# Parameter arithmetic at the head of the program, and S5's absolute phases in a half tile of their own, in a two-layer trunk of mixers and gated MLPs

## The chip, the cores and the metric

The kernel runs on one core of a Trainium2 chip. The metric is the device time of one execution in microseconds, taken as the median of several runs. One more execution was recorded by the hardware profiler; its trace gives the start and the length of each instruction. TensorE (PE) does matmuls and transposes, its weight loads are listed as PEld, VectorE is DVE, ScalarE is ACT, GpSimd is POOL, and SyncE (SP) issues nearly all DMAs.

## What is computed

The reference is a trunk of two layers on 1024 tokens of 1024 features, all in float32. Layer 0 mixes with RG-LRU (512 wide) and S5 (256 wide), layer 1 with HGRN2 and dilated attention, and each layer ends in a gated MLP with a short convolution. What the change touches are quantities of the parameters alone:

```python
# S5, per group and state
dt = jnp.exp(log_dt)[:, None]
mag = jnp.exp(ar * dt)
abar_re = mag * jnp.cos(ai * dt); abar_im = mag * jnp.sin(ai * dt)
# RG-LRU, per channel
log_a = (RG_C * r) * jax.nn.log_sigmoid(lam)
# HGRN2, per channel
lb_p = jax.nn.softmax(hg_lower, axis=0); lb_all = jnp.cumsum(lb_p, axis=0) - lb_p[0]
```

The S5 scan is done in blocks: the kernel forms cosines and sines of the phases `iota * angle` for 128 block positions, as sin(2 pi x) and sin(pi/2 - 2 pi |x|) of a phase x wrapped to half a turn either way.

## The kernel before

Tokens lie in 8 tiles of 128. In `load_x` SP issues the loads: a tile `par0` of all small parameters first, then the gain row, x tile by tile with weights in between, and S5's and RG-LRU's small weights. The small weights and the parameter results share wide tiles called arena, from which `tiny` hands out columns. One DVE instruction there needs no load (the memset of `ones`).

`start` then normalises the tiles. PE spreads the gain row over the partitions, DVE copies it out (L205, `gpre`), and each tile goes through a row sum of squares on ACT (L142), four dependent small DVE instructions for the reciprocal root (L134 to L137, behind L133), the product on DVE (L148, `xn`), 8 transposes on PE (L235, `pt`), and for each half a high part on ACT (L89, `yh`) and a low part on DVE (L90, `yl`). Projection matmuls (`pj`, L279 to L281) of the first two weight units run between the tiles. Inside `start` the order of PE, ACT and DVE is fixed by hand (`in_order`); everything else is ordered when the program is built, by a list scheduler that takes what it reckons to be ready, work that was traced earlier first. Once built, an engine runs its own list in order.

Three blocks of parameter arithmetic run on DVE, on 4 to 16 columns an instruction. `s5_params` begins with an exponential (`pexp`, 18 instructions, L766 to L778) for dt and the product t0 (L793), goes on with the exponential of t0 (mag) and the angles (th), then powers and tables. `rg_params` (L1036 to L1052) holds a `pexp` and a series for the logarithm. Both are traced behind the first part of the projections, and `hg_params` (L1366 to L1378, with a `pexp`) in layer 1. All three may not be issued on DVE ahead of the instruction that `self.dve_start` names, the last DVE instruction of the third tile's split (`tc.issue_after`).

Then `s5_lift` builds the tables of a quarter of S5's groups: products on POOL (L894 to L896), phase steps on DVE (L908 to L911 with `wrap`, L782 and L783), and on ACT Sin (L915), Abs in place (L916) and Sin (L917). There are four lifts. RG-LRU's convolution steps on DVE are L1061, and its gates use Sigmoid, Exp, Tanh and Sqrt on ACT; a change between some of these functions needs a table load on ACT.

Of the kernel before, what the change touches and what calls it, by code (L numbers as in the profile page):

```python
# [13 lines left out]
AF = mybir.ActivationFunctionType  # L14
ALU = mybir.AluOpType
# [30 lines left out]
class Trunk:  # L46
# [118 lines left out]
    def load_x(self, x, g):  # L165

        nc, a = self.nc, self.a
        self.hs = []
        self.par0 = self.small([P, 93], "par0", bufs=1)
        nc.sync.dma_start(self.par0, a["par0"])  # L170

        self.grow = self.T("grow")[:1]
        nc.sync.dma_start(self.grow, g.unsqueeze(0))
        self.ones = self.T("ones")[:1, :P]
        nc.vector.memset(self.ones, 1.0)
        self.gpre = self.cp.tile([P, 1024], F32, tag="g0", name="gpre")
        self.bx, self.cx = self.tiny("s5bx", 512), self.tiny("s5cx", 512)
        self.rgw, self.wglu = self.tiny("rgw", 1024), self.tiny("wglu", 512)
        for t in range(NT):
            if t % 2 == 0:  # L180
                h2 = self.T2("h")
            h = h2[:, t % 2]
            nc.sync.dma_start(h, x[t * P:(t + 1) * P, :])
            self.hs.append(h)
            if t == 0:
                nc.sync.dma_start(self.cst, a["cst"][:, :C_BIAS])
            if t == 1:
                self.fetch(2)
            if t == 5:
                nc.sync.dma_start(self.bx, a["s5_b"])  # L190
                nc.sync.dma_start(self.cx, a["s5_c"])
        nc.sync.dma_start(self.rgw, a["rg_w"])
        nc.sync.dma_start(self.wglu, a["s5_wglu"])
        self.rgw = self.rgw.rearrange("p (j c m) -> p j c m", j=2, c=4)
        self.wglu = self.wglu.rearrange("p (k c) -> p k c", k=2)

    def start(self):

# [586 lines left out]
    def s5_params(self):  # L785
        nc, a, v = self.nc, self.a, self.nc.vector
        tt = v.tensor_tensor
        G = 16
        par = self.par0
        ar, ai, ldt = par[:, 0:16], par[:, 16:32], par[:, 32:48]  # L790
        dt, mag, th, k, t0 = (self.tiny(f"s5{x}") for x in ("dt", "mag", "th", "k", "t0"))
        self.pexp(dt, ldt, 16)
        tt(t0, ar, dt, op=ALU.mult)  # L793
        self.pexp(mag, t0, 16)
        tt(th, ai, dt, op=ALU.mult)
        v.tensor_scalar(k, th, INV2PI, MAGIC, op0=ALU.mult, op1=ALU.add)
# [9 lines left out]
        sn, cs = self.tiny("s5sn"), self.tiny("s5cs")  # L806
# [12 lines left out]
        for m, n in ((1, 1), (2, 2), (4, 4)):  # L819
            br = pr[:, m:m + 1].to_broadcast([P, n, G])  # L820
            bi = pi[:, m:m + 1].to_broadcast([P, n, G])
            x, y = pr[:, 1:1 + n], pi[:, 1:1 + n]
# [57 lines left out]
    def s5_lift(self, q):  # L880

        nc, v = self.nc, self.nc.vector
# [22 lines left out]
        x, y = xy[:, 0], xy[:, 1]  # L905
# [6 lines left out]
        self.wrap(x, y)  # L912
        two = self.T2("s5csz")
        cs = w["cs"] = D4(two[:, 0])
        nc.scalar.activation(cs[:, 1], x, AF.Sin, scale=6.2831850)  # L915
        nc.scalar.activation(x, x, AF.Abs)  # L916
        nc.scalar.activation(cs[:, 0], x, AF.Sin, scale=-6.2831850, bias=self.halfpi)  # L917

        C1, C2 = (self.cx[:, j * 256:(j + 1) * 256].rearrange("p (g q) -> p g q", g=16) for j in range(2))
        z = w["z"] = D4(two[:, 1])  # L920
# [186 lines left out]
    def params0(self):  # L1107
        self.ahead(3)
        with self.tc.issue_after(self.dve_start):
            self.s5_params()  # L1110
            self.rg_params()
        self.gens.append([self.s5_all_tables(), 1])

    def s5_all_tables(self):
# [398 lines left out]
    def layer1_mixer(self, pend, hsrc, hdst):  # L1513
        nc = self.nc
        self.gens = []
        self.tick = self.drive(self.gens)
        self.qkv, self.og, self.ml, self.mix = {}, {}, {}, {}
        self.hq, self.ho, self.hsg = {}, {}, {}
        with self.tc.issue_after(self.dve_start):
            self.hg_params()  # L1520
        self.hg_values(pend)
        self.proj_chunks([self.da_job(g, kd, c) for g in range(3) for kd in "qkv" for c in range(2)], iter(pend), self.tick, parts=(512, 512))
        scm = self.T2("scm")
        self.scm = [scm[:, j].rearrange("p (t s) -> p t s", t=8) for j in range(2)]
        nc.gpsimd.memset(scm, 0.0)
        self.seg = self.cp.tile([P, 1024], F32, tag="g0", name="seg")
        nc.gpsimd.tensor_copy(self.seg.rearrange("p (n s) -> p n s", s=64), self.cst[:, C_SEG:C_SEG + 64].unsqueeze(1).to_broadcast([P, 16, 64]))

        jobs = [f(h) for h in range(4) for f in (self.hg_qjob, self.hg_fjob)] + [self.hg_gjob(h) for h in range(4)]
        self.proj_chunks(jobs, pend, self.tick, 4, (512, 512))  # L1530
        while self.gens:
            self.tick()
        return self.mix_out(1, 6, hsrc, hdst)
# [110 lines left out]
```

## Time and profile before

| | us |
|---|---|
| median of 3 runs | 2216.42 |
| lowest and highest | 2215.26, 2219.97 |
| profiled execution, its own time | 2214.25 |
| its span, first to last instruction | 2212.5 |
| PE busy | 2124.8 |
| DVE busy | 1589.3 |
| ACT busy | 1043.2 |
| POOL busy | 106.1 |

The busy times are sums over the span and lie beside one another. A stretch is read from the time of its own engines: one that is busy for the whole of it can set its length. In a timeline the distance from start to start is what an instruction takes of its engine's time; its own length can be longer, since the next may start before it has ended. The granted clock is the share of full speed that TensorE was given.

### The profile page before, as it was taken

To read this page: it belongs to the slowest core of one execution; us is meant where nothing else is said; L and a number is where in the kernel's file an instruction comes from. 1 tells how busy PE (TensorE), PEld (TensorE's weight loads), DVE (VectorE), ACT (ScalarE), POOL (GpSimd) and SP (SyncE) were. 2 spreads that over 40 slices of the span, in tenths; PEclk is the share of its full clock that TensorE was granted. 3 is DMA by queue.
4 is the path that set the end of the run, shared out by engine and by line. 5 is a ranking of instruction groups with operands and counts; after the bars stand their busy time and mean duration, and the time that the engine had idled before them with its cause. 6 is when DMAs were issued, how large, how long until landed. Compare 5 with 4: busy or idle time off the path is not lost.

```text
span 2212.5 us, 25422 instructions
## 1 busy us (share of the span) xinstructions
PE 2124.8 (96%) x10088; PEld 1720.5 (78%) x10088; DVE 1589.3 (72%) x2091; ACT 1043.2 (47%) x1437; POOL 106.1 (5%) x93
## 2 busy tenths in 40 slices
PE   7899989999999999999999999999899999999997
PEld 6677868888887888878877877778688888878886
DVE  8887687777777797971233366677877777778888
ACT  5548445444444444540233376444444544444443
POOL 0550000000000000000000000420000000000000
PEclk9999999999999999999999999999999999999999
DMA  4012322222213530330111111434122221234404
GB/s 164 12 35 98 116 103 86 78 85 86 86 71 119 211 140 23 116 141 29 39 34 54 47 35 29 118 112 157 53 86 86 86 86 70 83 141 163 153 10 152
DMA packets 53896, 198.82 MB, mean 90 GB/s; under 512 B 7045, under 2 KB 8133, under 8 KB 51218
## 3 DMA queue, kind: packets, MB, share of 16 engines
q1 hardware_dynamic: 52130, 193.49, 24.3%
q0 software_dynamic: 1504, 3.46, 0.6%
q8 instruction: 79, 1.29, 0.2%
q14 instruction: 39, 0.32, 0.0%
q10 hardware_dynamic: 144, 0.26, 0.0%
HBM read 154.60 MB, written 41.99 MB: 89 GB/s over the span
## 4 chain that ended last, share of the span: by engine, by line
PE 81%; DVE 12%; ACT 4%; issue 2%; DMA 1%; SPq 0%; DVEq 0%; ACTq 0%
PE ac L279 11%; PE ac L281 11%; PE ac L280 11%; PE pd L280 7%; PE pd L281 7%; PE pd L279 7%; PE pj L279 5%; PE pj L280 5%; PE pj L281 5%; PE bb L281 2%; PE bb L280 2%; PE bb L279 2%; DVE wl L90 1%; PE ppt L1263 1%; PE pi L281 1%
## 5 line engine op out<-in xcount | busy, mean ns | idle before, releaser
L279 PE MATMUL pj<-yh,wh 128*128 128x512 f32 (+1 forms) x672 | 267.5, 398 | 6.3 <-ACT s5uf L84 4.4
L280 PE MATMUL pj<-yl,wh 128*128 128x512 f32 (+1 forms) x672 | 262.0, 390 | 1.0 <-DVE yl L90 1.0
L281 PE MATMUL pj<-yh,wl 128*128 128x512 f32 (+1 forms) x672 | 260.2, 387 | 0.0
L280 PE MATMUL pd<-dwl,dgh 128*128 128x512 f32 x528 | 205.9, 390 | 0.8 <-DVE dwl L90 0.8
L281 PE MATMUL pd<-dwh,dgl 128*128 128x512 f32 x528 | 205.6, 389 | 0.0
L279 PE MATMUL pd<-dwh,dgh 128*128 128x512 f32 x528 | 205.3, 389 | 0.0
L279 PEld LDWEIGHTS pj<-yh,wh 128*128 128x128 f32 x672 | 129.7, 193 | 34.9 <-ACT s5uf L84 4.5
L279 PE MATMUL ac<-ah,w2h 128*128 128x512 f32 x352 | 143.8, 409 | 7.3 <-ACT ah L89 7.3
L280 PEld LDWEIGHTS pj<-yl,wh 128*128 128x128 f32 x672 | 129.6, 193 | 27.2 <-issue 4.1
L281 PEld LDWEIGHTS pj<-yh,wl 128*128 128x128 f32 x672 | 129.1, 192 | 24.7 <-issue 0.7
L279 PE MATMUL ac<-ah,w4h 128*128 128x512 f32 x352 | 142.2, 404 | 6.1 <-ACT val L489 3.8
L280 PE MATMUL ac<-al,w2h 128*128 128x512 f32 x352 | 139.4, 396 | 1.8 <-DVE al L90 1.8
L281 PE MATMUL ac<-ah,w2l 128*128 128x512 f32 x352 | 139.4, 396 | 0.0
L280 PE MATMUL ac<-al,w4h 128*128 128x512 f32 x352 | 137.6, 391 | 0.0
L281 PE MATMUL ac<-ah,w4l 128*128 128x512 f32 x352 | 137.3, 390 | 0.0
L280 PEld LDWEIGHTS pd<-dwl,dgh 128*128 128x128 f32 x528 | 99.1, 188 | 22.1 <-DVE dwl L90 1.6
L279 PEld LDWEIGHTS pd<-dwh,dgh 128*128 128x128 f32 x528 | 99.1, 188 | 20.8
L281 PEld LDWEIGHTS pd<-dwh,dgl 128*128 128x128 f32 x528 | 99.1, 188 | 20.4
L515 ACT ACTIVATE tg<-tg 128x1024 f32<-128x1024 f32 x44 | 46.7, 1061 | 137.9 <-DVE tg L448 137.9
L89 ACT ACTIVATE dwh<-dw 128x1024 fp32r<-128x1024 f32 x66 | 69.7, 1056 | 86.6 <-PE pd L280 72.8
L446 ACT ACTIVATE tv<-val,cw 128x1024 f32<-128x1024 f32 x44 | 54.7, 1243 | 108.8 <-DVE val L453 108.8
L90 DVE TENSOR_TENSOR w1l<-wr,w1h 128x1024 fp32r<-128x1024 f32 x44 | 53.9, 1225 | 64.1 <-ACT w1h L89 64.1
(444 smaller groups left out, 5023.4 us busy)
## 6 DMA issues: line engine op xcount, KB each, us to landing
wr<-in_WU_dram SPq DMA_DIRECT2D x88, 512.0 KB, 4.3
raw<-in_W_dram SPq DMA_DIRECT2D x56, 512.0 KB, 3.8
gd<-tv SPq DMA_DIRECT2D x44, 512.0 KB, 2.6
dg<-gd SPq DMA_DIRECT2D x20, 1024.0 KB, 5.2
dw<-in_WD_dram SPq DMA_DIRECT2D x20, 1024.0 KB, 7.9
h<-h SPq DMA_DIRECT2D x28, 512.0 KB, 4.2
h<-hn SPq DMA_DIRECT2D x20, 512.0 KB, 2.9
h<-in_x_dram SPq DMA_DIRECT2D x16, 512.0 KB, 4.9
```

Source lines behind the costliest of these rows:

```text
L89: self.nc.scalar.activation(hi, src, AF.Copy)
L90: self.nc.vector.tensor_tensor(lo, src, hi.bitcast(F32), op=ALU.subtract)
L279: mm(out, lhsT=lh, rhs=rh, start=first, stop=False, skip_group_check=chain)
L280: mm(out, lhsT=lh, rhs=rl, start=False, stop=False, skip_group_check=chain)
L281: mm(out, lhsT=ll, rhs=rh, start=False, stop=last, skip_group_check=chain)
L446: nc.scalar.activation(t0, src, AF.Identity, scale=cw[:, c, 2:3], bias=cw[:, c, 3:4])
L515: nc.scalar.activation(tg, tg, AF.Gelu_apprx_tanh)
L1263: nc.tensor.transpose(pt[:, hp, j], sc[:, hp, j], self.ident)
```

## The change

`load_x` now ends with dt's `pexp`, t0, `hg_params` and `rg_params`, on columns of the same arena, without the `issue_after`. They are traced ahead of `start` and are not part of its fixed order. `s5_params` takes dt and t0 from there, and `rgp` is set earlier since `rg_params` reads it. In `s5_lift` the Abs is traced first and writes into `y`, the half tile that the wrapping used before and that nothing needs any more; the two Sin follow, one of x and one of y.

```diff
--- before.py
+++ after.py
@@ -193,6 +193,13 @@
         nc.sync.dma_start(self.wglu, a["s5_wglu"])
         self.rgw = self.rgw.rearrange("p (j c m) -> p j c m", j=2, c=4)
         self.wglu = self.wglu.rearrange("p (k c) -> p k c", k=2)
+
+        dt, t0 = self.s5dt = self.tiny("s5dt"), self.tiny("s5t0")
+        self.pexp(dt, self.par0[:, 32:48], 16)
+        nc.vector.tensor_tensor(t0, self.par0[:, 0:16], dt, op=ALU.mult)
+        self.rgp = self.par0[:, 48:80].rearrange("p (c j) -> p c j", c=4)
+        self.hg_params()
+        self.rg_params()
 
     def start(self):
 
@@ -788,9 +795,8 @@
         G = 16
         par = self.par0
         ar, ai, ldt = par[:, 0:16], par[:, 16:32], par[:, 32:48]
-        dt, mag, th, k, t0 = (self.tiny(f"s5{x}") for x in ("dt", "mag", "th", "k", "t0"))
-        self.pexp(dt, ldt, 16)
-        tt(t0, ar, dt, op=ALU.mult)
+        mag, th, k = (self.tiny(f"s5{x}") for x in ("mag", "th", "k"))
+        dt, t0 = self.s5dt
         self.pexp(mag, t0, 16)
         tt(th, ai, dt, op=ALU.mult)
         v.tensor_scalar(k, th, INV2PI, MAGIC, op0=ALU.mult, op1=ALU.add)
@@ -912,9 +918,10 @@
         self.wrap(x, y)
         two = self.T2("s5csz")
         cs = w["cs"] = D4(two[:, 0])
+
+        nc.scalar.activation(y, x, AF.Abs)
         nc.scalar.activation(cs[:, 1], x, AF.Sin, scale=6.2831850)
-        nc.scalar.activation(x, x, AF.Abs)
-        nc.scalar.activation(cs[:, 0], x, AF.Sin, scale=-6.2831850, bias=self.halfpi)
+        nc.scalar.activation(cs[:, 0], y, AF.Sin, scale=-6.2831850, bias=self.halfpi)
 
         C1, C2 = (self.cx[:, j * 256:(j + 1) * 256].rearrange("p (g q) -> p g q", g=16) for j in range(2))
         z = w["z"] = D4(two[:, 1])
@@ -1108,7 +1115,6 @@
         self.ahead(3)
         with self.tc.issue_after(self.dve_start):
             self.s5_params()
-            self.rg_params()
         self.gens.append([self.s5_all_tables(), 1])
 
     def s5_all_tables(self):
@@ -1516,8 +1522,6 @@
         self.tick = self.drive(self.gens)
         self.qkv, self.og, self.ml, self.mix = {}, {}, {}, {}
         self.hq, self.ho, self.hsg = {}, {}, {}
-        with self.tc.issue_after(self.dve_start):
-            self.hg_params()
         self.hg_values(pend)
         self.proj_chunks([self.da_job(g, kd, c) for g in range(3) for kd in "qkv" for c in range(2)], iter(pend), self.tick, parts=(512, 512))
         scm = self.T2("scm")
```

## Rows read from the trace of the kernel before

**Rows 1.** The page's part 2, PE and DVE: busy tenths in 40 slices of 55.3 us.

```profile
PE   7899989999999999999999999999899999999997
...
DVE  8887687777777797971233366677877777778888
```

**Rows 2.** Three stretches: length, busy us of each engine (instructions), granted clock, DMA share, GB/s.

```profile
24.90:43.00 18.10, 14.07 (x115) 13.35 (x114) 18.10 (x130) 10.79 (x22) 0.00 (x0) 1.00 0.00 1
...
57.00:71.00 14.00, 11.50 (x61) 9.65 (x60) 14.00 (x26) 0.00 (x0) 12.48 (x11) 1.00 0.00 0
71.00:80.00 9.00, 6.04 (x24) 5.07 (x24) 6.85 (x9) 6.90 (x9) 2.69 (x5) 0.62 0.06 13
```

**Rows 3.** Waits from 20 to 60 us, PE: engine line <- who: us in total, times, longest.

```profile
PE pt L235 <- DVE xn L148: 6.2, 5, 2.6
```

**Rows 4.** Timeline, DVE, 21-43 us: start us, us, engine line op out<-in xcount [idle before <-releaser].

```profile
21.80 1.28 DVE L148 SCALAR_TENSOR_TENSOR xn<-h,rn,gpre 128x1024 f32<-128x1024 f32 x1
...
24.35 0.69 DVE L90 TENSOR_TENSOR yl<-pt,yh 128x512 fp32r<-128x512 f32 x1 [0.66 <-ACT yh L89]
24.96 0.17 DVE L766 TENSOR_SCALAR pe<-par 128x16 f32<-128x16 f32 x1
25.03 0.16 DVE L1366 TENSOR_TENSOR hgm<-par 128x4 f32<-128x4 f32 x1
...
26.70 1.28 DVE L148 SCALAR_TENSOR_TENSOR xn<-h,rn,gpre 128x1024 f32<-128x1024 f32 x1
...
36.32 1.28 DVE L148 SCALAR_TENSOR_TENSOR xn<-h,rn,gpre 128x1024 f32<-128x1024 f32 x1
...
42.73 0.16 DVE L1043 TENSOR_TENSOR arena<-arena 128x4 f32<-128x4 f32 x1
42.84 1.28 DVE L148 SCALAR_TENSOR_TENSOR xn<-h,rn,gpre 128x1024 f32<-128x1024 f32 x1
```

**Rows 5.** Timeline, DVE, 57 to 80 us.

```profile
57.30 0.15 DVE L1046 SCALAR_TENSOR_TENSOR arena<-arena 128x4 f32<-128x4 f32 x1
...
59.92 1.25 DVE L1046 SCALAR_TENSOR_TENSOR arena<-arena 128x4 f32<-128x4 f32 x1
...
61.90 1.27 DVE L1061 SCALAR_TENSOR_TENSOR rgu<-pj,par,rgu 128x1023 f32<-128x1023 f32 x1
...
70.39 0.30 DVE L1052 TENSOR_SCALAR arena<-arena 128x4 f32<-128x4 f32 x3
...
79.74 1.60 DVE L908 TENSOR_TENSOR s5x<-cst,arena 128x512 f32<-128x512 f32 x1
```

**Rows 6.** The parameters' tile (par): its DMA's issue, and its time to landing.

```profile
L170 SPq DMA_DIRECT2D par<-in_par_dram x1: 389/389/389, 0.7 to 0.7; - x1
...
DMA to landing us min/median/max: 1.8/1.8/1.8
```

**Rows 7.** Timeline, DVE, the opening.

```profile
6.47 1.23 DVE L205 COPY gpre<-pg 128x1024 f32<-128x1024 f32 x1 [5.42 <-PE pg L204]
...
7.86 0.16 DVE L135 TENSOR_TENSOR tn<-tn,vn 128x1 f32<-128x1 f32 x1
8.06 0.16 DVE L136 TENSOR_TENSOR tn<-tn,qn 128x1 f32<-128x1 f32 x1
```

**Rows 8.** Timeline, POOL, at 59.6 us.

```profile
59.60 1.54 POOL L896 TENSOR_TENSOR s5tm<-s5tm 128x512 f32<-128x512 f32 x1
```

**Rows 9.** Timeline, ACT, 87 to 96 us.

```profile
87.44 1.28 ACT L915 ACT_TABLE_LOAD   x1
89.11 0.64 ACT L915 ACTIVATE s5csz<-s5x 128x512 f32<-128x512 f32 x1 [0.38 <-DVE s5x L783]
...
92.21 0.61 ACT L916 ACTIVATE s5x<-s5x 128x512 f32<-128x512 f32 x1
...
93.88 1.28 ACT L917 ACT_TABLE_LOAD   x1
...
95.92 1.28 ACT L1079 ACT_TABLE_LOAD   x1
```

## The prediction

> **What bounds the kernel now.** I read the page's 40 slices first. A slice is 55 us. TensorE (PE) stands at 9 tenths or more nearly everywhere; of the slices with work of this change it is lower in the first two, with 7 and 8, while VectorE (DVE) stands at 8 in the first three [rows 1]. So in the opening some 110 us, and hardly behind them, a DVE instruction can be worth its time. Then I read the stretches. From 24.9 to 43 us DVE has no idle time at all (18.10 of 18.10) and PE works 14.07; from 57 to 71 us DVE is again full, 14.00 of 14.00, with PE at 11.50 [rows 2]. The waits between 20 and 60 us say who waits: PE's transposes wait five times, 6.2 us in all, for the DVE instruction that writes the normalised tile xn (L148) [rows 3]. So the path of these 50 us runs through DVE, and the small parameter instructions stand on it.
>
> **What the edit moves.** 86 DVE instructions: the exponential for dt (18) and t0 (1), hg_params (28), rg_params (39). No DMA moves, and nothing on SP's or POOL's queue. In the kernel before 72 of them start between 24.96 and 42.73 us [rows 4]; summing start to next start they take 6.03 us, 0.084 each. One more lies alone, and the last 13, the end of rg_params, lie from 57.30 to 70.39 us and take 5.39 us [rows 5]. The new place is the start of DVE's queue. The parameters' DMA is issued at 0.7 us and lands 1.8 us later [rows 6], at 2.5 us; DVE stands idle for 5.42 us until the gain row's copy into gpre (L205) starts at 6.47 [rows 7]. So 4.0 us of the hole can be used.
>
> **Term 1, the tiles of 25 to 43 us.** Not all of the 6.03 us comes back, since part of it filled holes. I take a tile's period from a stretch without these instructions: from one xn (21.80) to the end of the second yl (24.96, the idle 0.66 of the row at 24.35 included) is 3.16 us [rows 4], and the four dependent steps of a row's reciprocal root come at 0.20 each, 0.8 us [rows 7]. That makes 4.0 us. With the instructions it is 4.81 (26.70 to 36.32 is two periods) [rows 4]. Saved: 1.74 less 0.8 in the piece from 24.96 to 26.70, twice 0.8, and in the last period (36.32 to 42.84, 6.52 us, of which a weight's low part takes 1.22) 1.3. Sum **3.8 us**. S5's own chains of mag and th, some 25 instructions that stay, find the 0.66 us hole and the gaps of 0.12 us between dependent steps; if they find none, 25 x 0.08 = 2.0 us are lost again (lower end 1.8). The upper end is the whole 6.0. What is late next is PE itself: its 14.07 us are 4.0 short of the stretch [rows 2], which agrees with 3.8.
>
> **Term 2, the 13 instructions of 57 to 71 us.** Four of them, on 4 columns each, last over 1 us: the one at 59.92 takes 1.25 [rows 5], and ends at 61.17, when POOL's instruction of 59.60 ends (61.14) [rows 8]. So they wait for POOL to be done with something both use. If that wait passes on to the next DVE instruction, only 14 x 0.08 = 1.1 us are saved; if it goes with them, 5.4. For the first: in the second lift, where no small instruction stands in between, the phase product (L908) itself takes 1.60 us [rows 5]. For the second: here the first convolution's three steps (L1061) stand between the phase steps; the one at 61.90 reads 1023 columns from PSUM in 1.27 us [rows 5] while POOL works nearly throughout, 12.48 of 14 us [rows 2], so such steps can fill POOL's turns. I take **3.5**, somewhat nearer to this second end, for these three.
>
> **Term 3, S5's Abs ahead of both sines.** In lift 1 Sin, Abs and Sin are apart, with Exp and Tanh in between, and ScalarE (ACT) loads four tables, at 87.44, 93.88 and 95.92 us and once in between, 1.28 us each [rows 9]. With the absolute phases in their own half the second sine no longer waits on an Abs just issued, so the two sines can stand side by side: two loads fewer, 2.56 us. Against that, the first load (87.44) lay within a wait for DVE that lasted until 89.11 [rows 9]; Abs runs under any table here (92.21, behind an Exp and with no load of its own), so the load will come behind Abs, after the wait: 1.28 us given back. Net **1.3 us** on ACT, which works without a gap here from 89.11 to the load at 95.92 [rows 9]; ends 2.6 (the load stays hidden) and -1.3 (lifts 0 and 2, where the sines already stand together, gain nothing and only lose the hidden load). I credit nothing for lift 3.
>
> The Trainium skill (ScalarE: Activation LUTs, What ACT_TABLE_LOAD costs) puts a switch of sets at about 2.66 us, the load and a drain behind it; by that two switches are worth 5.3 us and the sum below would be 2.8 larger. The trace differs: the load at 93.88 and the Sin behind it leave room for the next load after 2.04 us (95.92) [rows 9], so there is no such drain.
>
> **Term 4, the opening.** DVE takes its instructions in queue order, so the change adds a wait: the gpre copy, the first reciprocal roots and the first xn are queued behind instructions that wait for the parameters' DMA, and PE's first transposes wait for xn. That wait is over at 2.5 us; what costs is the number of instructions ahead of the copy. Independent chains interleave at about 0.08 us an instruction (the 72 above at 0.084; 24.96 and 25.03) [rows 4]; one chain alone goes at 0.20 (7.86, 8.06) [rows 7]. Three chains are now ready at once. In the kernel before two such chains and a reciprocal root filled DVE without a hole, and the work ready earliest and traced earliest went first; here that is the three chains. So I expect the copy where the shortest chain ends: 3 x 19 = 57 instructions, 4.6 us, to 7.1 us: 0.6 late. The other 29 go into gaps of the first norms; I put another 0.6 for those that don't fit. **1.2 us lost.** Ends: 0 (49 or fewer are ahead: 49 x 0.08 = 3.9), and 4.6 if all 86 are ahead (19 rounds of 0.24, then 20 of 0.20, is 8.6 us, to 11.1).
>
> **Sum:** 3.8 + 3.5 + 1.3 - 1.2 = 7.4 us. All of it stands before 100 us. Behind it the work hangs together by engines and buffers and not by absolute times, so I carry it to the end whole. The profiled execution took 2214.25 us (span 2212.5, 1.75 around it), 2.2 below the median of 2216.42; I take 7.4 from the median: 2209.0.
>
> **Rivals.** (a) *The queue's head is slow: slower than before.* The 86 run chain by chain ahead of the copy: at the dependent 0.20 us they take 17.2 us, from 2.5 to 19.7, and the copy is 13.2 late; less the 8.6 of terms 1 to 3, 4.6 slower: 2221.0. It decides once the copy is later than 15 us. Against it: before, the dt and hg chains alternate one by one from the start [rows 4]. The Trainium skill (VectorE: DVE Perf Modes, The DRAIN you can't avoid) has a rule that speaks for it: a DVE instruction starts only when the one ahead has left the pipe. Here instructions of 0.16 to 0.17 us start 0.07 apart (24.96, 25.03) [rows 4], so independent ones overlap and the trace doesn't bear the rule out. Chance 0.09.
>
> (b) *Half of it is hidden anyway.* The lower ends of terms 1 and 2 with no gain on ACT and 1.2 lost: 1.8 + 1.1 - 1.2 = 1.7: 2214.7. For it: DVE's holes between yl halves are real, and in lift 1 the waits on POOL fall on whoever is there. Chance 0.19.
>
> (c) *It gives more: the clock too.* From 71 to 80 us the granted clock is 0.62, while PE works 6.04 of 9 us after idle time in the 14 us before [rows 2]; at full clock some 3.4 us of these 9 come back. With the upper ends of terms 1 and 2 halfway (4.9, 4.5) and term 3, less 1.2, plus 3.4: 12.9: 2203.5. Chance 0.20.
>
> (d) *The edit doesn't do what it says:* the moved instructions stay where they were because the queue puts the copy and the norms ahead of them. Then only term 3 is left: 2215.1. Against it: hg_params, traced only for layer 1, ran at 25.03 us [rows 4], as soon as it was allowed to. Chance 0.05.
>
> **How the numbers follow.** Forecast 2209.0, chance 0.47, with (a) to (d) as above. This kernel's measurement can tell about 0.2%, 4.4 us: faster means under 2212.0. Faster: the forecast and (c), 0.67. Same: (b) and (d), 0.24. Slower: 0.09. Range: all upper ends with the clock (6.0 + 5.4 + 2.6 + 3.4 = 17.4) reach 2199.0, all lower ends (1.8 + 1.1 - 1.3 - 4.6 = 3.0 lost) 2219.4; I take 2200 to 2218, which leaves out (a) and the corners.
>
> **What would show it.** Term 4: the start of L205's copy, 6.5 to 7.5 us, with some 57 small instructions ahead. Term 1: xn's periods at 4.0 to 4.2 us, the last xn near 40 us, and PE's 6.2 us of waits for L148 mostly gone. Term 2: the last phase step of lift 0 (L783, right behind the row at 70.39) 6 to 8 us earlier, and which instruction now lasts over 1 us while POOL works. Term 3: two Sin behind one load in lift 1. Wrong I would be if L205 starts beyond 11 us, if the lost time on POOL's turns reappears in full on the phases, or if the gain at 100 us is not there at 220.

## The result and the profile after

| | before | after |
|---|---|---|
| median, us | 2216.35 | 2229.84 |
| lowest and highest, us | 2215.26, 2219.97 | 2226.25, 2232.07 |
| profiled execution, its own time, us | 2214.25 | 2228.48 |
| its span, us | 2212.5 | 2226.7 |

The change makes the kernel slower: 1.0054 times the time of before, 95% interval 1.0043 to 1.0066, where 2209.0 us was forecast. The profiled executions differ by 14.2 us, and that is the sum to explain. Here is where it arises, as the start of the same instruction in both traces:

| start of | before, us | after, us | later by |
|---|---|---|---|
| the gain row's copy (gpre) | 6.47 | 7.51 | 1.0 |
| the first low part (yl) | 12.83 | 20.19 | 7.4 |
| the last of the eight xn | 42.84 | 51.32 | 8.5 |
| POOL's first product of lift 1 | 79.56 | 83.97 | 4.4 |
| the first gate's second Sigmoid | 86.31 | 102.59 | 16.3 |
| RG-LRU's first scan | 102.0 | 116.67 | 14.7 |
| the first matmul into pd, behind layer 0's mixers | 217.2 | 233.0 | 15.8 |
| the first gelu of the first MLP | 345.0 | 362.1 | 17.0 |
| the last row sum of the program (into hn) | 2200.6 | 2214.8 | 14.2 |

So 7.4 us are lost in the opening and 1.1 more up to the last xn, 4.1 are won between the last xn and lift 1, 11.9 are lost at one Sigmoid, and behind 100 us the lateness moves by 3 us at most. First the page's part 2, PE and DVE in 40 slices, to be read beside [rows 1]:

```profile
PE   6889989999999999999999999899899999999997
DVE  7787688777777797981234257677877777778888
```

PE's first slice falls from 7 to 6, and the rest hardly moves. Then stretches, with the columns of [rows 2]; the first is the tiles (24.9 to 43 us there, moved on by 8.5), the second the one behind POOL:

```profile
33.40:51.50 18.10, 14.37 (x107) 13.82 (x105) 14.24 (x58) 11.04 (x22) 0.00 (x0) 0.91 0.00 1
...
65.00:79.00 14.00, 12.06 (x64) 10.15 (x62) 13.93 (x17) 2.33 (x5) 13.01 (x12) 1.00 0.00 0
```

DVE's work in the tiles fell from 18.10 to 14.24 us with 72 instructions fewer (58 instead of 130), by about what Term 1 forecast as saved time, and the tiles take no less than before: DVE is now idle for the difference. PE's waits between 20 and 60 us for xn, 6.2 us in [rows 3], are mostly still there:

```profile
PE pt L242 <- DVE xn L148: 5.0, 3, 2.8
```

(Three are left of five, also when the window is moved on by 8.5 us; at two of the tiles PE itself comes late, which the section on the prediction takes up.)

**The opening**, DVE's timeline, against [rows 7]:

```profile
2.56 0.17 DVE L773 TENSOR_SCALAR pe<-par 128x16 f32<-128x16 f32 x1 [1.51 <-DMA par<-in_par_dram]
...
7.43 0.17 DVE L1384 TENSOR_SCALAR oml<-lb 128x4 f32<-128x4 f32 x1
7.51 1.22 DVE L212 COPY gpre<-pg 128x1024 f32<-128x1024 f32 x1
...
13.85 0.17 DVE L785 TENSOR_TENSOR arena<-pe,peki 128x16 f32<-128x16 f32 x1
13.94 0.16 DVE L1043 TENSOR_SCALAR arena<-par 128x4 f32<-128x4 f32 x1
...
18.34 1.54 DVE L1053 SCALAR_TENSOR_TENSOR arena<-arena 128x4 f32<-128x4 f32 x8
...
20.19 0.68 DVE L90 TENSOR_TENSOR yl<-pt,yh 128x512 fp32r<-128x512 f32 x1
```

DVE begins when the parameters land, at 2.56 us as [rows 6] gave it, and the chains of dt and hg run before the copy (45 instructions; the heads of three chains, 57, were forecast). But dt's last step, the first that writes to the arena (13.85), stands behind two xn and a weight's low part, and behind it, in front of the first yl, t0 and 36 of the 39 instructions of rg_params: from 13.94 to 20.19 us DVE works through what is nearly one dependent chain, at 0.20 us a step. ACT waits for it 7.49 us:

```profile
20.91 0.60 ACT L89 ACTIVATE yh<-pt 128x512 fp32r<-128x512 f32 x1 [7.49 <-DVE yl L90]
```

One row of SP's queue says what is special about the arena: a weight that lies in the same tile is loaded late, the last of that tile's loads.

```profile
12.75 0.33 SPq L193 DMA_DIRECT2D arena<-in_s_wglu_dram  x1
```

**Lift 1**, ACT's timeline, against [rows 9]:

```profile
87.95 1.11 ACT L1078 ACTIVATE rgg<-rgpg,par 128x1024 f32<-128x1024 f32 x1 [3.92 <-PE rgpg L1076]
98.10 0.63 ACT L922 ACTIVATE s5x<-s5x 128x512 f32<-128x512 f32 x1 [9.03 <-DVE s5x L790]
98.75 1.28 ACT L923 ACT_TABLE_LOAD   x1
100.04 0.63 ACT L923 ACTIVATE s5csz<-s5x 128x512 f32<-128x512 f32 x1
100.58 0.70 ACT L924 ACTIVATE s5csz<-s5x,halfpi 128x512 f32<-128x512 f32 x1
101.30 1.28 ACT L1078 ACT_TABLE_LOAD   x1
102.59 1.11 ACT L1078 ACTIVATE rgg<-rgpg,par 128x1024 f32<-128x1024 f32 x1
```

Abs and the two Sin stand together behind one load, as forecast. They also stand between the gate's two Sigmoids, and ACT is idle 9.03 us until DVE has the phases. In the kernel before, both Sigmoids came first:

```profile
84.53 1.11 ACT L1071 ACTIVATE rgg<-rgpg,par 128x1024 f32<-128x1024 f32 x1 [4.66 <-PE rgpg L1069]
86.31 1.11 ACT L1071 ACTIVATE rgg<-rgpg,par 128x1024 f32<-128x1024 f32 x1 [0.67 <-PE rgpg L1069]
```

And the phases themselves got later: their first product takes 4.78 us where [rows 5] have 1.60, and they end at 98.06 us. Behind the Sigmoid the gate's product on DVE waits 5.08 us for it, and the first scan follows. DVE's timeline of after:

```profile
83.91 4.78 DVE L914 TENSOR_TENSOR s5x<-cst,arena 128x512 f32<-128x512 f32 x1
...
97.37 0.69 DVE L790 TENSOR_TENSOR s5x<-s5x 128x512 f32<-128x512 f32 x1
...
103.74 1.23 DVE L1081 TENSOR_TENSOR rgg<-rgg,rgu 128x1024 f32<-128x1024 f32 x1 [5.08 <-ACT rgg L1078]
...
116.67 2.29 DVE L1090 TENSOR_TENSOR_SCAN rgg<-rgg,rgt 128x1024 f32<-128x1024 f32 x1
```

In the kernel before the phases end at 89.08 us:

```profile
87.41 1.67 DVE L783 TENSOR_TENSOR s5x<-s5x 128x512 f32<-128x512 f32 x1
...
102.02 2.29 DVE L1083 TENSOR_TENSOR_SCAN rgg<-rgg,rgt 128x1024 f32<-128x1024 f32 x1
```

### The profile page after: what moved, and what is told of

Read it like the earlier page. It is cut to its first block, busy times and chain, and to the rows that moved or that the text cites. A ratio compares the mean times of both kernels' runs of the same rounds, so it can differ in the third digit from the quotient of the medians.

```text
span 2226.7 us, 25418 instructions
## 1 busy us (share of the span) xinstructions
PE 2127.5 (96%) x10088; PEld 1722.2 (77%) x10088; DVE 1597.3 (72%) x2091; ACT 1043.1 (47%) x1437; POOL 103.5 (5%) x93
## 4 chain that ended last, share of the span: by engine, by line
PE 80%; DVE 13%; ACT 5%; issue 2%; DMA 1%; DVEq 0%; ACTq 0%; SPq 0%
PE ac L286 11%; PE ac L288 11%; PE ac L287 11%; PE pd L287 7%; PE pd L286 7%; PE pd L288 7%; PE pj L287 5%; PE pj L286 5%; PE pj L288 5%; PE bb L288 2%; PE bb L286 2%; PE bb L287 2%; DVE wl L90 1%; PE ppt L1269 1%; PE pi L288 1%
```

## The experiments

The theory from the two traces: (A) the second Sigmoid is late because lift 1's three activations stand ahead of it on ACT and wait for DVE; (B) the opening is late because results share a tile with a late load, so they are placed behind it and in front of yl. Rivals: the moved instructions cost by their number; or the Abs edit costs by itself.

All runs in one table: starts against the kernel before in the profiled executions, us later (negative is earlier); the median against the one of before on the same chip; the ratio with its 95% interval. No kernel leaves work out.

| kernel | first yl | last xn | lift 1, POOL | 2nd Sigmoid | first scan | first pd | first gelu | last hn | median | ratio |
|---|---|---|---|---|---|---|---|---|---|---|
| after | 7.4 | 8.5 | 4.4 | 16.3 | 14.7 | 15.8 | 17.0 | 14.2 | +13.5 | 1.0054 [1.0043, 1.0066] |
| abs_only | 0.1 | 0.9 | 0.1 | 12.7 | 11.0 | 12.6 | 12.4 | 12.3 | +11.1 | 1.0044 [1.0029, 1.0059] |
| par_only | 7.5 | 8.3 | 4.3 | 12.4 | 9.4 | 12.6 | 12.7 | 16.5 | +11.0 | 1.0043 [1.0029, 1.0057] |
| rg_back | 1.3 | 1.4 | 1.1 | 13.7 | 12.1 | 11.7 | 11.7 | 12.0 | +9.8 | 1.0041 [1.0023, 1.0059] |
| late_sin | 7.5 | 8.2 | 6.6 | 6.0 | 6.9 | 8.1 | 9.5 | 12.8 | +10.3 | 1.0042 [1.0025, 1.0059] |
| abs_late | 0.1 | 0.1 | 2.0 | 1.7 | 3.5 | 3.6 | 7.2 | 7.7 | +6.0 | 1.0024 [1.0013, 1.0035] |
| rg_own | 0.0 | 1.0 | -2.4 | 5.1 | 2.2 | 3.3 | 5.1 | 2.0 | +4.2 | 1.0021 [1.0012, 1.0031] |
| rg_own_late | 0.1 | 1.1 | 0.5 | 2.2 | -1.3 | 2.1 | 2.1 | 2.3 | +3.6 | 1.0017 [1.0006, 1.0027] |
| own_tile | 3.2 | 3.8 | -0.2 | 11.7 | 10.1 | 11.6 | 11.7 | 8.2 | +5.9 | 1.0028 [1.0019, 1.0038] |
| late1 | 0.1 | 0.6 | 2.3 | 1.8 | -1.7 | 4.1 | 7.6 | 4.9 | +4.1 | 1.0020 [1.0010, 1.0029] |
| abs_late1 | 0.1 | 0.9 | 1.9 | 2.1 | 3.4 | 5.0 | 5.1 | 5.3 | +3.9 | 1.0019 [1.0009, 1.0028] |
| rg_own_late1 | 0.0 | 0.8 | -1.7 | -2.9 | -4.1 | 1.1 | 4.5 | -1.6 | +0.5 | 0.9998 [0.9989, 1.0008] |
| own_tile_late1 | 3.1 | 4.1 | 0.0 | -1.0 | 0.7 | 3.8 | 5.4 | 5.3 | +2.9 | 1.0007 [0.9995, 1.0018] |
| abs_lateq1 | 0.1 | 0.9 | 1.9 | 2.2 | 3.4 | 4.9 | 8.3 | 8.9 | +5.3 | 1.0027 [1.0015, 1.0038] |
| rg_own_lateq1 | 0.1 | 1.5 | -1.1 | -3.8 | -3.5 | -2.7 | -1.0 | -0.4 | -2.0 | 0.9991 [0.9982, 1.0001] |
| rg_own_abs_lateq1 | 0.2 | 0.3 | -2.3 | -2.5 | -4.5 | -3.3 | 0.2 | 4.4 | -1.8 | 0.9993 [0.9984, 1.0003] |
| own_tile_lateq1 | 3.1 | 3.1 | -0.9 | -0.3 | 0.6 | 1.7 | 3.1 | 6.2 | +1.3 | 1.0003 [0.9994, 1.0013] |

Each row of starts is one execution. The last column of starts differs from the first gelu's by 6.1 us less to 4.2 more within one kernel's trace; this comes in layer 1, between 1270 and 1480 us, and goes with no edit. The column of the first gelu holds up to 3.6 us that come from the clock and not from the edit (last section). The columns up to the first pd carry the argument.

### Each half of the change, and each half undone

abs_only is the kernel before with the change's three activation lines; par_only has all of the change but these; rg_back and late_sin are the changed kernel with one move taken back or one added:

```diff
 # rg_back: after, with rg_params at its old place
-        self.rg_params()            # in load_x
             self.s5_params()
+            self.rg_params()
 # late_sin: after, the three activations issued in s5_tables
-        nc.scalar.activation(y, x, AF.Abs)          # ... and both Sin, in s5_lift
+        w["xy"] = x, y
+        nc.scalar.activation(y, x, AF.Abs)          # ... and both Sin, in s5_tables
```

> The kernel before with the Abs alone changed (into the other half tile, ahead of both Sin); the parameters stay where they were. Theory A: what costs is ACT's queue. In the order built, the Abs and both Sin of lift 1 stand ahead of the second gate's Sigmoid and wait for DVE's phases; before, that Sigmoid ran at 86.3 us and the phases were ready at 89.1, so it comes at about 89.1 + 0.6 + 1.3 + 1.3 + 1.3 = 93.6, 7 us late: 2222 to 2225. Theory B (ACT only saves loads, the loss is all in the opening): 2215, and the Sigmoid at 86 to 88.

> The changed kernel with Sin, Abs in place, Sin as they were before; the parameters moved. Theory A: opening 7.4 us late as in the changed kernel, some 4 us won back between 52 and 82 us, and since the first Sin of lift 1 still stands ahead of the second Sigmoid in the order built, some 4 to 7 more are lost there: 2223 to 2228. Theory B (only the opening counts): 2216.4 + 7.4 - 4 = 2220.

> The changed kernel with rg_params back at its old place behind s5_params; dt, t0 and hg_params stay moved, the Abs stays ahead. Opening theory: the first yl comes at 14 us and not at 20.2, as rg_params' chain no longer stands ahead of it; the last xn at 44 us and not 51.3. Theory A then still loses some 7 us at lift 1: 2223 to 2226. Theory B (the opening is all): 2217 to 2218.

> The changed kernel with each lift's three activations traced with its tables, behind the gates, and nothing else changed: in the order built both Sigmoid of the first gates now stand ahead of lift 1's Abs. Theory A: opening 7.4 us late, 4 won back by 82 us, the second Sigmoid right behind the first: 2219 to 2222. Rival (the late Sigmoid is a consequence and not a cause, DVE's phases behind POOL set the time): still 2228 to 2231.

The two halves lose 11.1 and 11.0 us alone and 13.5 together, since either of them makes the second Sigmoid late. abs_only loses 12.6 us between lift 1's start (0.1 late) and the second Sigmoid (12.7), which is enough for its 11.1 us of median; 7 were expected, and the rest is phases that end 5.4 us later. par_only and rg_back fall within theory A's times. abs_only's ACT timeline shows the same queue as after, with no parameter moved:

```profile
85.63 1.11 ACT L1072 ACTIVATE rgg<-rgpg,par 128x1024 f32<-128x1024 f32 x1 [5.32 <-PE rgpg L1070]
94.47 0.63 ACT L916 ACTIVATE s5x<-s5x 128x512 f32<-128x512 f32 x1 [7.73 <-DVE s5x L783]
...
98.97 1.11 ACT L1072 ACTIVATE rgg<-rgpg,par 128x1024 f32<-128x1024 f32 x1
```

par_only has the old order of the three, and its second Sigmoid is 12.4 late all the same, 8.1 of them behind lift 1's start: here the first Sin alone stands between the Sigmoids. So the Abs is not needed for the fault: moving parameters alone can turn the two round when the program is built. By what reckoning the scheduler does it is not traced. rg_back takes the opening's loss from 7.4 to 1.3 and puts rg_params' instructions back among the tiles: its DVE is busy for 16.08 of the 18.1 us from 24.9 (80 instructions, against 58 in after). From the fourth xn to the last it takes 21.1 us (23.13 to 44.26), before takes 21.0, and own_tile_lateq1 (below), without those instructions and with PE as early there as in before, 21.0 as well (24.92 to 45.90): their number costs nothing there. late_sin frees the Sigmoid, which comes 6.0 late instead of 16.3, and still gains only 3.2 us of median: it also loses the 2.2 us by which lift 1 now starts later, so the test was not clean, and its 2226.3 lies between the times of the theory and of the rival.

### The tile, and the queue

abs_late and rg_own_late issue the activations with the transposes in every lift, as late_sin does, from the kernel before; rg_own and own_tile move results out of the arena:

```diff
 # rg_own (from before) and own_tile (from after)
-        w, s, q, p = (self.tiny(f"rg{j}", 4) for j in range(4))
+        w, s, q, p = (self.small([P, 4], f"rg{j}", bufs=1) for j in range(4))
 # (the same for cc, ncc, cc2; own_tile for dt and t0 as well)
```

> The kernel before with the Abs ahead of both Sin as in the change, and each lift's three activations traced with its tables, behind the gates; the parameters stay. In the order built both Sigmoid of the first gates stand ahead of lift 1's Abs. Theory A (the loss of the Abs edit is the second Sigmoid behind the Abs): the second Sigmoid at 86 to 88 us, the first scan at 102 to 105, 2214 to 2220. Rival (the Abs ahead costs by itself, its load no longer hidden): 2222 or more.

> The kernel before with rg_params' results in small tiles of their own instead of arena columns; nothing is moved in the program. In the order built its chain begins right behind the third tile's split, at 25 us instead of 34.9, and is done before POOL starts. Term 2 alone: the second lift's POOL work starts 3 to 5 us earlier than 79.6. Theory A: the first Sin of lift 1 now stands ahead of the second Sigmoid in the order built, which comes at 93 to 99 us: 2218 to 2224. Rival (no such loss): 2211 to 2213.

> As rg_own, and the activations of each lift traced with its tables, in their old order Sin, Abs, Sin; both Sigmoid of the first gates stand ahead of lift 1's first Sin. Theory A with term 2: 3 to 5 us won at 80 us and kept: 2211 to 2214. Rival (what DVE wins ahead of 80 us is lost behind POOL in lift 1 whatever ACT's order is): 2216 to 2220.

> The changed kernel with dt, t0 and rg_params' results in small tiles of their own instead of columns of the arena that the last small weight is loaded into. Theory on the opening: in the changed kernel these instructions had to come behind that load's issue at 12.75 us in the order built; without it 70 or more of the 86 come ahead of the gain row's copy, which starts at 9.5 to 11 us instead of 7.5, and the first yl follows at 16 to 17.5 instead of 20.2. The second Sigmoid stays behind the Abs: 2225 to 2228. Rival (the chain of rg_params is served late for another reason): first yl at 20 again.

own_tile settles (B): the opening's loss falls from 7.4 to 3.2 us with every instruction still there, and the median by 7.6, to 2222.0, below the 2225 to 2228 expected. What is left of it is the copy, which now stands behind 75 of the 86 instructions:

```profile
8.94 0.17 DVE L1051 TENSOR_SCALAR rg<-rg 128x4 f32<-128x4 f32 x1
9.14 0.36 DVE L1053 SCALAR_TENSOR_TENSOR rg<-rg,rg 128x4 f32<-128x4 f32 x2
9.42 1.22 DVE L212 COPY gpre<-pg 128x1024 f32<-128x1024 f32 x1
```

rg_own needs no change of order in the opening: with tiles of their own the rg_ instructions leave the stretch behind POOL by themselves, and lift 1 starts 2.4 us earlier. Then the first Sin stands ahead of the second Sigmoid, which is 5.1 late, and the gain is gone: 4.2 us slower than before by the median, within theory A's times. abs_late and rg_own_late have both Sigmoids ahead of lift 1 as meant, but their times, 2222.0 and 2219.7, are those of their rivals. In both lift 0's activations are late too, and lift 1 starts 2.0 and 0.5 us late where abs_only started it 0.1 late and rg_own 2.4 early: they price a second thing beside the Sigmoid, and late issue in lift 0 is dropped from here on.

### Lifts 1 to 3 late, lift 0 as it was

```diff
+        def sines():                  # the three activations of the kernel in question
+        w["sines"] = sines
+        if q == 0:
+            w.pop("sines")()          # s5_lift
+        if q:
+            w.pop("sines")()          # s5_tables, ahead of the transposes
```

> The kernel before with one edit: the three activations of lifts 1 to 3 (Sin, Abs, Sin in the old order) issued with the lift's transposes instead of with its phases. No work left out. It prices this place of issue by itself: the theory of queue order says that in the kernel before the second Sigmoid already stood ahead of the first Sin, so the front gains nothing: first gelu within 1.5 us of the kernel before, time 2214 to 2219. Rival (issuing them later costs by itself, because the lift's own matmuls wait for the sines): first gelu 2 to 6 us late, time 2218 to 2223.

> The kernel before with the Abs edit alone (Abs ahead of both sines, into the other half of the tile; abs_only took 2227.1 us, second Sigmoid 12.7 us late) and, as in the run beside it, the three activations of lifts 1 to 3 issued with the lift's transposes. No work left out. Theory queue order: the Abs edit itself costs nothing and saves two table loads of 1.28 us per lift; the second Sigmoid is within 1.5 us of the kernel before, time 2211 to 2217, that is 1 to 4 us below the run with the late issue alone. Rival (the Abs edit costs by itself, whatever the queue): first gelu 7 to 12 us late, time 2222 to 2227.

> The kernel before with two edits: the rg_ results in small tiles of their own (rg_own, 2220.2 us: lift 1 started 2.4 us earlier, second Sigmoid 5.1 us later) and the three activations of lifts 1 to 3 (Sin, Abs, Sin in the old order) issued with the lift's transposes. No work left out. Theory queue order: the 2.4 to 4.3 us won ahead of the gate stay won, the second Sigmoid starts 2 to 4 us earlier than in the kernel before, the first gelu of the first FFN is 0 to 4 us earlier, time 2210 to 2217. Rival A: the first gelu is 4 to 6 us late as in rg_own, time 2219 to 2222.

> own_tile (the changed kernel with dt, t0 and the rg_ results in small tiles of their own; 2222.0 us, second gate Sigmoid 11.7 us late) with one more edit: in lifts 1 to 3 the three activations (Abs, Sin, Sin) are issued with the lift's transposes instead of with its phases; lift 0 as it was. No work left out. Theory queue order (the changed kernel's main loss is lift 1's activations standing ahead of the second gate's Sigmoid in ScalarE's queue): the second Sigmoid starts within 2 us of the kernel before, the first FFN's first gelu is under 4 us late instead of 11.7, and the time is 2211 to 2218. Rival A (the sines are needed where they were, so the time only moves behind them): the gate's Sigmoid is early but the scans of both gates or the first FFN are still 8 to 12 us late, time 2220 to 2224. Rival B (tail of layer 1, whose time differs from one execution to the next, takes back what the front wins): first gelu under 4 us late, time 2218 to 2222.

Against own_tile, own_tile_late1 has the second Sigmoid 12.7 us and the first pd 7.8 us earlier; that is (A) by itself. Its time is 1 us above the range for queue order and its first gelu 5.4 late instead of under 4: from the first scan (0.7 late) on it loses 4.7 us, 1.6 of them by the clock, which no theory had, and neither rival's numbers fit either. rg_own_late1 came as expected in time but not at the first gelu (4.5 late, 3.4 of it by the clock). late1 went as its rival said in time: issuing late costs 4 us by itself (its first gelu, 7.6 late, is later than the rival's 2 to 6, by 3.5 us of clock). Against it abs_late1 is at -0.2 us: with the queue free the Abs edit neither costs nor wins anything that the end shows, though its first scan is 5.1 us later, and both numbers given for it were missed.

Of the 2.3 us that late1 loses before lift 1, 1.8 are [rows 5]' price again: the three small instructions that took 0.30 us there now last 2.12, while POOL works.

```profile
70.87 2.12 DVE L1060 TENSOR_SCALAR arena<-arena 128x4 f32<-128x4 f32 x3
```

### Lift 1 alone late

The same with `q != 1` and `q == 1`: lifts 2 and 3 are issued as in the changed kernel (abs, own_tile) or in that of before.

> The kernel before with the Abs edit (Abs ahead of both sines into the other half of the tile) and lift 1's three activations alone issued with its transposes; lifts 0, 2 and 3 as in abs_only. No work left out. Theory (the loss of abs_only, 11 us, is the second gate's Sigmoid behind lift 1's activations and nothing else): second Sigmoid within 2.5 us of the kernel before, first gelu of the first FFN 0 to 3 us late, time 2214 to 2219. Rival A (the 4 us that all runs with late issue lost between 115 and 205 us come from lift 1's late issue itself): first gelu 4 to 6 us late, time 2219 to 2222. Rival B (the Abs edit in lifts 2 and 3 costs by itself): first gelu over 6 us late, time over 2222.

> The kernel before with the rg_ results in small tiles of their own and lift 1's three activations alone (old order Sin, Abs, Sin) issued with its transposes; beside it rg_own_late1, which issued those of lifts 2 and 3 late too, took 2216.6 us. No work left out. Theory: the first scan 4 us early as there, and what it lost from 115 to 205 us (5 us) goes: first gelu 0 to 4 us early, time 2210 to 2215. Rival A (lift 1's late issue costs those 5 us): first gelu 4 to 5 us late, time 2215 to 2219.

> As rg_own_lateq1, with the Abs edit in all lifts: the two gains forecast ahead of the second Sigmoid (4.1 and 1.3 us) without the late Sigmoid and with the opening as it was. No work left out. Theory (both terms were sound, and the Sigmoid ate them): first gelu 1 to 5 us early, time 2208 to 2214. Rival A (what comes after 115 us is bound by something that neither reaches): first gelu within 2 us of the kernel before, time 2214 to 2218. Rival B (the Abs edit costs by itself): time over 2219.

> The changed kernel with dt, t0 and the rg_ results in small tiles of their own and lift 1's three activations alone issued with its transposes; own_tile_late1, which issued those of lifts 2 and 3 late too, took 2219.0 us, own_tile 2222.0. No work left out. Theory: the opening costs 3 to 4 us, the stretch behind POOL gives them back, the Sigmoid is free: first gelu 0 to 4 us late, time 2214 to 2219. Rival A (lift 1's late issue itself costs 4 to 5 us): first gelu 5 to 6 us late, time 2218 to 2221.

In rg_own_lateq1 and rg_own_abs_lateq1 both Sigmoids are ahead of lift 1's activations, the first scan is 3.5 and 4.5 us early and layer 0's mixers end 2.7 and 3.3 us early. ACT's timeline of the latter:

```profile
82.08 1.11 ACT L1079 ACTIVATE rgg<-rgpg,par 128x1024 f32<-128x1024 f32 x1 [4.41 <-PE rgpg L1077]
83.86 1.12 ACT L1079 ACTIVATE rgg<-rgpg,par 128x1024 f32<-128x1024 f32 x1 [0.67 <-PE rgpg L1077]
84.88 1.14 ACT L1086 ACTIVATE rgt<-rgg,rgc 128x1024 f32<-128x1024 f32 x1
86.92 0.63 ACT L917 ACTIVATE s5x<-s5x 128x512 f32<-128x512 f32 x1 [0.90 <-DVE s5x L783]
```

By the median 2.0 and 1.8 us are left of it, inside what the measurement can tell; these are the best kernels of the study, and neither is shown to beat the one before. For the former the theory's numbers hold (2210 to 2215, first gelu 1.0 early); for the latter rival A's do, though not its reason, since the 3.3 us are there at the first pd and go behind it (last section). abs_lateq1 missed its theory's time: it is at +5.3 us, abs_late1 at +3.9, and the two intervals overlap. Its first pd is as late (4.9 against 5.0), so issuing lifts 2 and 3 late had cost abs_late1 nothing, whereas in the old order of the three it did (rg_own_late1 loses 5.2 us from the first scan to the first pd, rg_own_lateq1 0.8). The other 3.4 us it loses on the way to the first gelu, by the clock. own_tile_lateq1, the whole change with both faults mended, is at +1.3 us, as its theory said: not slower than before any more, and not faster.

One distance shows the price of ACT's order by itself, since neither the opening nor the phases' turns with POOL are in it: from the end of lift 1's phases on DVE to RG-LRU's first scan.

| ACT's order | kernels | phases' end to first scan, us |
|---|---|---|
| both Sigmoids, then Sin, Abs, Sin | before | 12.9 |
| Sigmoid, Sin, Sigmoid | par_only, rg_own | 14.8 |
| Sigmoid, Abs, Sin, Sin, Sigmoid | after, abs_only, rg_back, own_tile | 18.6 |
| both Sigmoids, Sin issued late | late1; rg_own_late, rg_own_late1, rg_own_lateq1 | 8.9; 8.7 |
| both Sigmoids, Abs ahead of Sin, issued late | abs_late, late_sin, abs_late1, own_tile_late1, abs_lateq1, own_tile_lateq1, rg_own_abs_lateq1 | 10.7 |

The kernels of a row agree to 0.03 us (late1 aside), whatever else they change. So the order of after costs 5.7 us up to the scan, and the Abs ahead of Sin costs 3.8 us with the Sigmoids apart and 1.9 with both ahead. In after the first scan's 14.7 us are 4.4 at lift 1's start, 4.6 by longer phases and 5.7 by this order. (Issuing late shortens this distance and can lose it again behind the scan: late1 loses 5.8 us from there to the first pd.)

## Why the prediction was wrong, step by step

**What bounds the kernel** was read rightly as far as the engine went and wrongly as to what it waits for. DVE had no idle time in the tiles [rows 2], but that did not make its instruction count the bound.

**Term 1 (3.8 us) failed.** The step: "That makes 4.0 us", a tile's period without the small instructions. In the trace of after it is 4.70 (39.92 to 44.62), against 4.81 before, and over the tiles not even these 0.1 us a tile came back. DVE's timeline has the parts:

```profile
39.92 1.28 DVE L148 SCALAR_TENSOR_TENSOR xn<-h,rn,gpre 128x1024 f32<-128x1024 f32 x1
41.12 0.68 DVE L90 TENSOR_TENSOR yl<-pt,yh 128x512 fp32r<-128x512 f32 x1
42.47 0.69 DVE L90 TENSOR_TENSOR yl<-pt,yh 128x512 fp32r<-128x512 f32 x1 [0.66 <-ACT yh L89]
43.50 0.15 DVE L133 TENSOR_SCALAR vn<-ss 128x1 f32<-128x1 f32 x1 [0.34 <-ACT xn L142]
...
44.62 1.29 DVE L148 SCALAR_TENSOR_TENSOR xn<-h,rn,gpre 128x1024 f32<-128x1024 f32 x1
```

and ACT's, in the same period:

```profile
41.84 0.60 ACT L89 ACTIVATE yh<-pt 128x512 fp32r<-128x512 f32 x1 [2.25 <-DVE yl L90]
42.33 1.05 ACT L142 ACTIVATE xn<-h 128x1024 f32<-128x1024 f32 x1
43.28 0.19 ACT L142 ACTIVATION_READ_ACCUMULATOR xn<-h 128x1 f32 x1
```

From xn to the end of the second yl are 3.24 us, as the prediction had it (3.16). From there to the next xn are 1.46, not 0.8: the root's steps can start only at 43.50, when ACT has the next tile's row sum; ACT begins it behind the second high part, and that high part waits 2.25 us for DVE's first low part. The period is a round trip, DVE to ACT and back, and the small instructions had filled its holes on DVE. The prediction took the root's four steps as its price and did not ask what they wait for.

**Term 2 (3.5 us) held**: 4.1 us, from 8.5 late at the last xn to 4.4 at lift 1. rg_own shows it without the opening: 1.0 late at the last xn, 2.4 early at lift 1, 3.4 us; three later runs with the same edit give 2.6. The four waits of over 1 us went with the instructions, as the second end had it, but not all of the waiting: in after a copy (66.21, 1.33 us) and lift 0's last phase step (75.06, 1.75) are long while POOL works, where in before they are not.

**Term 3 (1.3 us) had the wrong sign.** The step "two loads fewer" failed: the two Sin do stand behind one load, but ACT has 60 loads in the trace of before and 60 in after's, since the gates' functions, torn apart, load again (Sigmoid at 101.30, 108.14 and 115.40 us). With both Sigmoids ahead the edit leaves 57 or 58, and as many as without it ahead of the first scan; there it costs 1.9 us, the Abs (0.63) and the load that is no longer hidden (1.28), which the prediction had counted as given back. (The 2.8 us that the prediction gives beside this term leave that load at 1.28; with one price for all three loads they would be 1.4.) The larger part that was left out is that the new order of three activations is a new order of ACT's queue: [rows 9] had Sin waiting for DVE until 89.11 with both Sigmoids already done, and nothing but the order built held them ahead. 11.9 us were lost at the second Sigmoid, in after as in abs_only (12.6); of these 4.6 are phases that end 14.1 us behind POOL's first product (83.97 to 98.06) instead of 9.5 (79.56 to 89.08), and 7.3 the Sigmoid's place, 4.5 us behind the phases' end instead of 2.8 ahead of it. The 11.9 are not this term's alone: in par_only, with the old order of the three, the moved parameters lose 8.1 there. Neither end of the term (2.6, -1.3) asked who is queued behind the moved instruction. That was asked for Term 4 alone, where it was in plain sight.

**Term 4 (1.2 us) was too small.** The copy came 1.0 late (0.6 forecast), behind two chains and not three; the last steps of hg's ran alone at 0.20 us. "The other 29 go into gaps of the first norms" failed: 38 instructions, 36 of them rg_params', came ahead of the first yl at the pace of one chain, 6.3 us, 7.4 with the copy and beyond the upper end of 4.6. The prediction's premise "No DMA moves, and nothing on SP's or POOL's queue" was true and beside the point: the results are written to a tile into which a late load of SP's goes.

**The rivals.** (a), which ends slower, was given 0.09. Its mechanism, a chain at the dependent pace ahead of the tiles' work, is what happened, at the first yl and not at the copy, so that its sign "the copy is later than 15 us" would have missed it. Its 2221.0 lacks the Sigmoid. (b) was right about DVE's holes between the yl halves and alone would not have made it slower. (c), the clock, came without its gain: the nine us that answer to the 0.62 of [rows 2] have 1.00, with PE busy 6.50 us instead of 6.04,

```profile
75.40:84.40 9.00, 6.50 (x40) 5.67 (x40) 7.02 (x8) 6.69 (x9) 6.10 (x8) 1.00 0.06 13
```

and no engine is busy for the whole of it; what the stretch waits for is not traced. (Its 3.4 us were also too many: at full clock PE's 6.04 busy us would give back 2.3.) (d) is excluded: the instructions moved.

The sum as it was: 7.4 in the opening and 1.1 more in the tiles, less 4.1, plus 11.9 at the Sigmoid, are 16.3 us late at 102.6 us, against 7.4 early forecast; 14.2 at the end. The 1.1 come between the fourth and the fifth xn, where PE is late: its projection matmuls follow one another at 0.21 us up to 29.4 us (0.12 from 31.7 on), and ACT waits 3.25 us for the transposes behind them (2.06 in before). abs_only, which moves no parameter, loses 0.8 us in the same place with the same pace, so the moved instructions are not the cause; the granted clock reads 1.00 there, and what sets this pace stays open.

## What to carry to other kernels

Before crediting a moved or reordered instruction, write down the queue of its engine as it will be built, and ask for each one behind it who waits: one activation that waits 9 us for another engine, as here, holds up all that stand behind it for as long, however short it is. An engine without idle time may still be paced by a round trip to another, so take a period from its longest chain of waits and not from its instruction count. And results that share a tile with a late load are ordered with that load; give them a tile of their own before moving them ahead.

## What the runs showed of the hardware

**One DVE instruction can wait through several of POOL's.** The product at 83.91 (4.78 us; the one of lift 0 at 65.61 takes 0.68) ends at 88.69, and POOL's timeline of after shows it passed over by six instructions in a row:

```profile
83.97 1.13 POOL L900 TENSOR_TENSOR s5tm<-arena 128x512 f32<-128x512 f32 x1
85.03 1.12 POOL L901 TENSOR_TENSOR s5tm<-arena 128x512 f32<-128x512 f32 x1
...
87.82 0.31 POOL L902 TENSOR_TENSOR s5zt<-s5zt 128x64 f32<-128x64 f32 x1
88.21 1.44 POOL L901 TENSOR_TENSOR s5zt<-arena 128x512 f32<-128x512 f32 x1
```

In the kernel before, the same product started 0.18 us behind POOL's first (79.74 and 79.56) and took 1.60. It went as in after in own_tile (4.83), and in rg_own the step behind the product was passed over by five (4.38). In the three traces in which the product starts 0.18 to 0.25 us behind POOL's first (before, late1, rg_own_abs_lateq1) lift 1's phases end 9.5 to 9.6 us behind that start; in the other fifteen, where a DVE instruction starts up to 0.6 us ahead of POOL's first, they end 11.3 to 14.8 behind it. Starting first does not always lose: in lift 0 of after the product starts 0.01 us ahead of a POOL instruction (65.61 and 65.62) and it is POOL's that gets longer (1.63). No run varies the order of starts alone, so what decides stays open. The Trainium skill (SBUF — State Buffer, Terms) has DVE and GpSimd arbitrate for one pair of ports that is held for a whole instruction while the loser fully blocks; the trace agrees in that the product ends 0.56 us behind the end of POOL's sixth (88.13), and shows beyond it that the loser can lose six times running.

**The granted clock at the start of the first MLP differs between runs that do the same.** PE's timeline, first of the kernel before, then of rg_own_abs_lateq1:

```profile
298.12 0.50 PE L281 MATMUL ac<-ah,w1l 128*128 128x512 f32 x1 [1.54 <-DVE vn L133]
```

```profile
294.86 0.80 PE L281 MATMUL ac<-ah,w1l 128*128 128x512 f32 x1 [1.54 <-DVE vn L133]
```

Both come behind the same two idle times, 1.14 and 1.54 us. From there to the next transposes PE took 5.12 us (to 303.24) in the one and 7.93 (to 302.79) in the other. The stretches (columns as in [rows 2]) have the clock at full, 2.4 GHz, in the kernel before and at about half, the 1.2 GHz level, in the other:

```profile
298.10:306.00 7.90, 7.05 (x34) 5.75 (x35) 7.87 (x16) 1.51 (x3) 0.00 (x0) 1.00 0.22 67
```

```profile
294.80:301.00 6.20, 6.14 (x15) 4.84 (x16) 6.17 (x14) 0.94 (x2) 0.00 (x0) 0.51 0.20 59
```

So 2.8 of the 3.5 us that this kernel loses between the first pd and the first gelu lie in this stretch at half the clock. All 18 traces fall into three groups. In the 6.2 us that begin 9.9 us behind the first matmul into ac the granted clock is 1.00 in seven, 0.72 to 0.75 in six and 0.50 to 0.51 in five, and from the first pd to the first gelu these take 127.6 to 127.9, 129.1 to 129.6 and 131.2 to 131.4 us. No edit goes with the groups (before, par_only and own_tile are in the first, after and rg_own in the second, late1 and abs_lateq1 in the third), so up to 3.6 us at the first gelu say nothing on an edit. Why the clock fell in one and not in the other, and whether layer 1 varies for the same reason, stays open.
